# Odd layer of a hybrid decoder trunk: TensorE's order fixed as written, wider distances in the inversion, top priority for the recurrence

## The chip, the cores and the metric

The kernel runs on one core of one Trainium2 chip. The metric is device time in microseconds (us) of one launch. The kernel before takes 2293.18 us (median of 3 runs, 2288.69 to 2293.35). A difference of 0.2%, about 4.6 us, is what can be told from no change here.

## The reference

The model is a two-layer trunk on a sequence of 1024 tokens with 1024 channels. Layer 0 (even) holds dilated attention and an HGRN2 recurrence; the change does not touch it. Layer 1 (odd) is a gated DeltaNet: a projection to q, k (8 heads of 128) and v (16 heads of 128), a causal convolution over 4 steps and SiLU, then the chunked delta rule, a gated RMS norm and an output projection.

```python
def gated_delta_rule_chunked(q, k, v, g, beta):
    ...
    lower = jnp.where(strict, jnp.einsum('bhnid,bhnjd->bhnij', kb, kc) * decay, 0.0)
    a_mat = lower + jnp.eye(C_CHUNK, dtype=jnp.float32)
    sol = lax.linalg.triangular_solve(a_mat, rhs, left_side=True, lower=True, unit_diagonal=True)
    ...
    def step(state, inp):
        u_n, w_n, a_n, qd_n, kt_n, gl_n = inp
        v_new = u_n - jnp.einsum('bhcd,bhdv->bhcv', w_n, state)
        o = jnp.einsum('bhcd,bhdv->bhcv', qd_n, state) + jnp.einsum('bhij,bhjv->bhiv', a_n, v_new)
        new_state = state * gl_n[..., None, None] + jnp.einsum('bhcd,bhcv->bhdv', kt_n, v_new)
        return new_state, o
```

For each k head and each chunk a unit lower triangular matrix is inverted, and then a recurrence runs over the chunks. The kernel uses chunks of 128 tokens, so 8 of them, and does the two v heads that share a k head together.

## The kernel before

The odd layer works through 8 heads. Three kinds of work belong to a head `hh`:

- **Projections, the fill.** `proj(j)` yields the output gate of head j-2 (`way_out`, tiles `oz`, from j = 2 on), and the convolved projections of k of head j+1 (`pk`, absent for j = 7), v of head j (two, `pv`) and q of head j (`pq`). Each projection has two halves of 512 tokens; a half is 24 matmuls on TensorE, then a chain of ScalarE and VectorE passes (`conv`, lines 822 to 831: copy, scale, three multiply-adds, tanh, one more multiply-add). Transposes (`tk`, `tq`, `tv`, `ot`) follow half a projection later. A step of fill is 6 matmuls and is counted in the code as 1.3.
- **Inversion.** `invert(hh)` computes k times k transposed in two parts (`kk`, line 986), turns them into `L` on VectorE (line 992) with decays that ScalarE makes, and inverts the 32 by 32 diagonal blocks on VectorE: a transpose `Lp` (line 1001), 31 dependent pairs of passes `tm` and `Tp` (lines 1007 and 1009), the transposes `Tn` and `Un` (lines 1011 and 1013). Then six small groups of matmuls put the blocks together: `qp`, `up`, two of `q2` (shown as `q`, line 1053) and two of `u2` (shown as `u`, line 1061), each with a copy from PSUM between it and the next.
- **Recurrence.** `recur(hh)` has three parts for a chunk: `ks` and `qs` (matmuls with the state) with the passes `r` on VectorE and `oq` on ScalarE; `vp` with `vt` on VectorE and `vn` on ScalarE; `kv`, `op` and the next chunk's `qk` with the state `S`, `A` and `bv` on VectorE. Each part needs the one before it.

Python generators weave these together. `mix(recur(hh), fill, 2.8)` puts steps of fill worth 2.8 between two parts of the recurrence, and `blend(invert(hh + 1), fill, 0.8)` puts steps worth 0.8 times a written distance between the parts of the next head's inversion. The distance is the first number of each `yield` in `invert`. So, while the recurrence of head hh runs, the projections and the inversion of head hh+1 are the fill.

This fixes the order in which instructions are emitted, and that is only a preference. The framework's scheduler orders each engine's queue when the program is built: of the instructions that are ready by its own estimate of the time, it takes the one that was emitted first. In the attention of the even layer TensorE's order is already kept as emitted, by a region `tc.manual_schedule(engines={PE})`; in the odd layer it is not.

PSUM banks are shared by tag: two for projections (`pj`), two for transposes (`a`), two for `ks`, `kv` and `op` (`b`), one for the inversion's results (`c`) and one for `qk`, `qs` and `vp` (`d`).

The start of the layer is special. `invert(0)` is woven into the end of the gates and `proj(0)` and is emitted before the first head's loop.

Of the kernel before, what the change touches and what calls it, by code (L numbers as in the profile page):

```python
# [9 lines left out]
F32 = mybir.dt.float32  # L10
F32R = mybir.dt.float32r
BF16 = mybir.dt.bfloat16
I32 = mybir.dt.int32
AF = mybir.ActivationFunctionType
ALU = mybir.AluOpType
# [63 lines left out]
def trunk_kernel(ctx: ExitStack, tc: tile.TileContext, x, ew, ewo, ow, owab, owo, nw, fnw, lbl, hnw,  # L79
# [11 lines left out]
    def bank(tag, shape, name):  # L91
        return pp.tile(shape, F32, name=name, tag=tag, bufs=BANKS[tag])
# [79 lines left out]
    def drain(fill):  # L172
        for _ in fill:
            pass
# [565 lines left out]
    def odd_layer(es):  # L740
# [199 lines left out]
        def way_out(hh):  # L940
            normed(hh)
            w = unit()
            for e in range(2):
                yield from gate(hh, w, e, lambda h, g: gated(hh, e, h, g))
# [22 lines left out]
        def invert(hh):  # L967
# [14 lines left out]
            for h in range(2):  # L982
                kk = bank("c", [P, 4, 128], f"kk{hh}_{h}")
                for c in range(4 * h, 4 * h + 4):
                    k_ = kT[:, c * 128:(c + 1) * 128]
                    pe.matmul(kk[:, c - 4 * h, :], k_, k_, start=True, stop=True)
                for c in range(4 * h, 4 * h + 4):
                    gcB = ahead_l.pop()
                    if c < NT - 1:
                        ahead_l.append(decay_l(c + 1))  # L990
                    for e in range(2):
                        dve.scalar_tensor_tensor(L[:, 2 * c + e, :], kk[:, c - 4 * h, :], SC[hh][:, 0, c, e:e + 1],
                                                 gcB[:, e, :], op0=ALU.mult, op1=ALU.mult)
                yield (15 if h else 7.0), 0.9


            for b in range(4):
# [32 lines left out]
                    pe.matmul(qp[a0[r], u, :], L[b0[r], u, a0[r]], Un[b0[r], u, :], start=True, stop=True)  # L1030
            act.copy(Q_[a0[0], :, 0:32], qp[a0[0]])
            dve.tensor_copy(Q_[a0[1], :, 0:32], qp[a0[1]])
            yield 1.5, 1.3
            up = bank("c", [P, 16, 32], f"up{hh}")
            for u in range(16):
                for r in range(2):
# [8 lines left out]
                r = slice(32 * b, 32 * b + 32)  # L1045
                pool.tensor_copy(U[r, :, r], Un[r])

            yield 2.0, 1.8
            for h in range(2):

                q2 = bank("c", [P, 4, 64], f"q2{hh}_{h}")
                for u in range(8 * h, 8 * h + 8):
                    pe.matmul(q2[u % 2 * 64:u % 2 * 64 + 64, u // 2 % 4, :], L[64:128, u, 0:64], U[64:128, u, 64:128],
                              start=True, stop=True)
                for e in range(2):
                    (act.copy if h ^ e else dve.tensor_copy)(Q_[0:64, 8 * h + e:8 * h + 8:2, :], q2[64 * e:64 * e + 64])
                yield 1.2, 1.7
            for h in range(2):
                u2 = bank("c", [P, 4, 64], f"u2{hh}_{h}")
                for u in range(8 * h, 8 * h + 8):  # L1060
                    pe.matmul(u2[u % 2 * 64:u % 2 * 64 + 64, u // 2 % 4, :], T64[:, u, :], Q_[0:64, u, :], start=True, stop=True)
                for e in range(2):
                    d = U[0:64, 8 * h + e:8 * h + 8:2, 64:128]
                    if h ^ e:
                        act.mul(d, u2[64 * e:64 * e + 64], -1.0)
                    else:
                        dve.tensor_scalar(d, u2[64 * e:64 * e + 64], -1.0, None, op0=ALU.mult)
                yield 1.2, 1.7
            dve.memset(U[64:128, :, 0:64], 0.0)
            US[hh] = U  # L1070

        def recur(hh):

            kT, kn, q, bv, U = KT[hh], KN[hh], Q[hh], BV[hh], US[hh]
            ss = SS[hh] = sp.tile([P, NT, 2], F32, name=f"oss{hh}", tag="oss", bufs=2)

            def decay_a(c):
                DA = decays(hh, c, "a")
                pool.tensor_tensor(DA, DA, MA[:, None, :].to_broadcast([P, 2, 128]), op=ALU.add)
                for e in range(2):  # L1080
                    act.activation(DA[:, e, :], DA[:, e, :], AF.Exp, bias=gt["ngc"][:, c, 2 * hh + e:2 * hh + e + 1])
                return DA

            def attend(c):

                DA = ahead_a.pop()
                if c < NT - 1:
                    ahead_a.append(decay_a(c + 1))
                qk = bank("d", [P, 128], f"qk{hh}_{c}")
                s = slice(c * 128, (c + 1) * 128)  # L1090
                pe.matmul(qk, kT[:, s], q[:, s], start=True, stop=True)
                A = sp.tile([P, 2, 128], F32, name=f"A{hh}_{c}", tag="A", bufs=2)
                dve.tensor_tensor(A, qk[:, None, :].to_broadcast([P, 2, 128]), DA, op=ALU.mult)
                return A

            ahead_a = [decay_a(0)]
            yield 1.0
            A = attend(0)
            St = None
            for c in range(NT):  # L1100
                col = [slice(2 * hh + e, 2 * hh + e + 1) for e in range(2)]
                s = slice(c * 128, (c + 1) * 128)
                if c:
                    ks = bank("b", [P, 2, 128], f"ks{hh}_{c}")
                    pe.matmul(ks, kT[:, s], St, start=True, stop=True)
                    r_ = sp.tile([P, 2, 128], F32, name=f"r{hh}_{c}", tag="r")
                    for e in range(2):
                        dve.scalar_tensor_tensor(r_[:, e, :], ks[:, e, :], SC[hh][:, 1, c, e:e + 1],
                                                 bv[:, c, e, :], op0=ALU.mult, op1=ALU.add)
                    qs = bank("d", [P, 2, 128], f"qs{hh}_{c}")  # L1110
                    pe.matmul(qs, q[:, s], St, start=True, stop=True)
                    oq = sp.tile([P, 2, 128], F32, name=f"oq{hh}_{c}", tag="oq")
                    for e in range(2):
                        act.activation(oq[:, e, :], qs[:, e, :], AF.Copy, scale=gt["eg"][:, c, col[e]])
                else:
                    r_ = bv[:, 0]
                yield 1.0
                vp = bank("d", [P, 2, 128], f"vp{hh}_{c}")
                for e in range(2):
                    pe.matmul(vp[:, e, :], U[:, 2 * c + e, :], r_[:, e, :], start=True, stop=True)  # L1120
                if c < NT - 1:
                    vt = sp.tile([P, 2, 128], F32, name=f"vt{hh}_{c}", tag="vt")
                    dve.tensor_tensor(vt, vp, gt["etl"][:, c, 2 * hh:2 * hh + 2, None].to_broadcast([P, 2, 128]), op=ALU.mult)
                vn = sp.tile([P, 2, 128], F32, name=f"vn{hh}_{c}", tag="vn")
                act.copy(vn, vp)
                yield 1.0
                if c < NT - 1:
                    kv = bank("b", [P, 2, 128], f"kv{hh}_{c}")
                    pe.matmul(kv, kn[:, c, :], vt, start=True, stop=True)
                    Sn = sp.tile([P, 2, 128], F32, name=f"S{hh}_{c}", tag="S", bufs=2)  # L1130
                    if c:
                        for e in range(2):
                            dve.scalar_tensor_tensor(Sn[:, e, :], St[:, e, :], gt["egl"][:, c, col[e]],
                                                     kv[:, e, :], op0=ALU.mult, op1=ALU.add)
                    else:
                        dve.tensor_copy(Sn, kv)
                    St = Sn
                op = bank("b", [P, 2, 128], f"op{hh}_{c}")
                for e in range(2):
                    pe.matmul(op[:, e, :], A[:, e, :], vn[:, e, :], start=True, stop=True)  # L1140
                A = attend(c + 1) if c < NT - 1 else None
                if c:
                    dve.tensor_tensor(bv[:, c], op, oq, op=ALU.add)
                else:
                    dve.tensor_copy(bv[:, c], op)
                for e in range(2):
                    jk = sp.tile([P, 128], BF16, name=f"oj{hh}_{c}_{e}", tag="jk", bufs=2)
                    act.activation(jk, bv[:, c, e, :], AF.Square, accum_out=ss[:, c, e:e + 1])
                yield 1.0


# [29 lines left out]
        def seq(*gs):  # L1181
            for g in gs:
                yield from g
# [6 lines left out]
        while 0 not in KN:  # L1190
            next(fill)
        drain(blend(invert(0), fill, 0.8))
        for hh in range(8):
            fill = proj(hh + 1) if hh < 7 else seq(way_out(6), gate7(), out_last(range(3), ["pj"]))
            if hh < 7:
                fill = blend(invert(hh + 1), fill, 0.8)
            mix(recur(hh), fill, 2.8)
            drain(fill)
        nwf = sp.tile([P, D], F32, name="nwf", tag="ub")
        load_row(nwf, fnw)  # L1200
        drain(blend(way_out7(), out_last(range(3, 8), ["pj", "b"])))
# [68 lines left out]
```

## Time and profile before

| what | value |
|---|---|
| median of 3 runs | 2293.18 us |
| the profiled execution | 2290.27 us, span 2288.5 us |
| TensorE busy | 2171.9 us (95%) |
| VectorE busy | 1427.0 us (62%) |
| ScalarE busy | 963.4 us (42%) |
| granted TensorE clock, mean | 0.993 |

The profiled execution lies 2.9 us under the median of the runs. Its span leaves 1.8 us of its own time outside. The odd layer's head loop fills the stretch from about 1294 to 2135 us. In the views, PE is TensorE, DVE is VectorE, ACT is ScalarE; names of tiles appear without their numbers; a window row gives its start and end, its length, then busy time and number of instructions of PE, PEld (weight loads), DVE, ACT and POOL, then the granted TensorE clock, the DMA share and GB/s.

### The profile page before, as it was taken

How to read it: one execution, taken by the hardware profiler on the slowest of the kernel's cores; microseconds unless marked ns; L12 is line 12 of the kernel's file. 1: busy time of each engine (PE TensorE's matmuls, PEld its weight loads, DVE VectorE, ACT ScalarE, POOL GpSimd, SP SyncE). 2: the span in 40 equal slices, each digit the busy share in tenths (PEclk: the TensorE clock that was granted, in tenths of full speed). 3: DMA queues.
4: the chain of work that ended last, by engine and by line, in shares of the span. 5: the costliest groups of instructions: out<-in, count | busy, mean ns of one | idle time of the engine just before them, and what ended most of it. 6: DMA issues, size and time to landing. Idle time of an engine off the chain costs nothing. (4 is left out here: it accounts for less than half of the span.)

```text
span 2288.5 us, 54642 instructions
## 1 busy us (share of the span) xinstructions
PE 2171.9 (95%) x22597; PEld 1809.0 (79%) x22597; DVE 1427.0 (62%) x3364; ACT 963.4 (42%) x2623; POOL 226.5 (10%) x236
## 2 busy tenths in 40 slices
PE   7999999999999999988999988989899989899998
PEld 6888888898888888866887776767777767678787
DVE  6444444444444444456777887878788877855777
ACT  5333333333333332322236663755555555544223
POOL 0000000000000000000000012131212121210000
PEclk9999999999999999999999998999999999999999
DMA  4111111113222323352323221121212121214232
GB/s 145 38 48 48 44 47 48 43 39 95 78 82 84 90 83 92 97 160 88 102 97 104 59 56 62 53 79 46 76 43 76 52 74 59 65 60 148 91 113 109
DMA packets 101864, 175.83 MB, mean 77 GB/s; under 512 B 16752, under 2 KB 34032, under 8 KB 101616
## 3 DMA queue, kind: packets, MB, share of 16 engines
q1 hardware_dynamic: 101616, 172.35, 24.2%
q8 instruction: 177, 2.90, 0.5%
q14 instruction: 71, 0.58, 0.1%
HBM read 127.07 MB, written 25.23 MB: 67 GB/s over the span
## 5 line engine op out<-in xcount | busy, mean ns | idle before, releaser
L113 DVE TENSOR_TENSOR w_lo<-raww,w_hi 128x512 fp32r<-128x512 f32 x292 | 211.9, 727 | 151.1 <-ACT w_hi L112 147.1
L112 ACT CAST w_hi<-raww 128x512 fp32r<-128x512 f32 x292 | 181.1, 620 | 270.1 <-PE op L145 68.0
L143 PE MATMUL av<-w_hi,hn_hi 128*128 128x256 f32 x512 | 149.0, 291 | 0.0
L143 PE MATMUL bi<-w_hi,hn_hi 128*128 128x256 f32 x512 | 147.0, 287 | 0.0
L144 PE MATMUL bi<-w_lo,hn_hi 128*128 128x256 f32 x512 | 145.3, 284 | 0.0
L144 PE MATMUL av<-w_lo,hn_hi 128*128 128x256 f32 x512 | 144.8, 283 | 0.0
L145 PE MATMUL bi<-w_hi,hn_lo 128*128 128x256 f32 x512 | 144.8, 283 | 0.0
L145 PE MATMUL av<-w_hi,hn_lo 128*128 128x256 f32 x512 | 144.7, 283 | 0.0
L575 ACT ACTIVATE P<-P,nm 128x256 f32<-128x256 f32 (+7 forms) x128 | 71.4, 559 | 130.2 <-DVE nm L573 130.0
L143 PE MATMUL op<-w_hi,yplo 128*128 128x512 f32 x288 | 113.5, 394 | 1.6 <-DVE hr L273 0.9
L145 PE MATMUL op<-w_hi,yplo 128*128 128x512 f32 x288 | 112.2, 390 | 0.0
L144 PE MATMUL op<-w_lo,yplo 128*128 128x512 f32 x288 | 112.1, 389 | 0.0
L143 PE MATMUL pv<-hn_hi,w_hi 128*128 128x512 f32 x256 | 107.0, 418 | 2.6 <-ACT uv L822 2.6
L143 PE MATMUL oz<-hn_hi,w_hi 128*128 128x512 f32 x256 | 109.4, 427 | 0.0
L273 DVE TENSOR_TENSOR hr<-hr,op 128x512 f32<-128x512 f32 x128 | 86.1, 684 | 34.5 <-PE op L145 34.0
L145 PE MATMUL pv<-hn_hi,w_lo 128*128 128x512 f32 x256 | 104.3, 407 | 0.0
L144 PE MATMUL pv<-hn_lo,w_hi 128*128 128x512 f32 x256 | 102.6, 401 | 0.0
L144 PE MATMUL oz<-hn_lo,w_hi 128*128 128x512 f32 x256 | 102.3, 400 | 0.0
L145 PE MATMUL oz<-hn_hi,w_lo 128*128 128x512 f32 x256 | 102.0, 398 | 0.0
L581 DVE STREAM_TRANSPOSE PB<-P 128x256 f32<-128x256 f32 (+3 forms) x64 | 54.6, 854 | 74.9 <-ACT P L575 74.8
L143 PEld LDWEIGHTS av<-w_hi,hn_hi 128*128 128x128 f32 x512 | 97.9, 191 | 3.5 <-issue 1.9
L144 PEld LDWEIGHTS bi<-w_lo,hn_hi 128*128 128x128 f32 x512 | 98.1, 192 | 0.0
(354 smaller groups left out, 6044.9 us busy)
## 6 DMA issues: line engine op xcount, KB each, us to landing
raww<-in_ew_dram SPq DMA_DIRECT2D x128, 256.0 KB, 3.1
raww<-in_ow_dram SPq DMA_DIRECT2D x100, 256.0 KB, 3.0
V<-v SPq DMA_DIRECT2D x256, 64.0 KB, 2.0
rawy<-ymix SPq DMA_DIRECT2D x64, 256.0 KB, 2.7
raww<-in_ewo_dram SPq DMA_DIRECT2D x32, 256.0 KB, 3.0
gcl<-gcd SPq DMA_DIRECT2D x64, 128.0 KB, 3.0
gca<-gcd SPq DMA_DIRECT2D x64, 128.0 KB, 3.0
ymix<-oy SPq DMA_DIRECT2D x32, 256.0 KB, 2.0
```

What stands on the lines that cost most here:

```text
L112: act.copy(hi, raw)
L113: dve.tensor_tensor(lo, raw, hi.bitcast(F32), op=ALU.subtract)
L143: pe.matmul(ps, lh, rh, start=start, stop=False)
L144: pe.matmul(ps, lh, rl, start=False, stop=False)
L145: pe.matmul(ps, ll, rh, start=False, stop=stop)
L273: dve.tensor_tensor(dst[:, n], src[:, n], ps, op=ALU.add)
L575: act.activation(Pm[:, e, w0:], Pm[:, e, w0:], AF.Exp, bias=nmx[:, e:e + 1], scale=0.125, accum_out=den[:, i, e:e + 1])
L581: dve.transpose(PB[:, :, i * WG + w0:(i + 1) * WG], Pm[:, :, w0:])
```

## The change

Three edits, all in the odd layer. The number and the shapes of the instructions stay the same.

1. The loop over the heads is put into a region in which TensorE issues its instructions as emitted. The other engines remain the scheduler's. `invert(0)` and what comes before it stay outside.
2. The distances in `invert` grow from 7, 15, 1.5, 2, 1.2 (four times) to 10, 45, 4, 4, 3 (four times).
3. The three parts of each chunk of the recurrence are emitted at the highest priority, so that on the other engines they go ahead of whatever else is ready.

```diff
-                yield (15 if h else 7.0), 0.9
+                yield (45.0 if h else 10.0), 0.9
...
-            yield 1.5, 1.3
+            yield 4.0, 1.3
...
-            yield 2.0, 1.8
+            yield 4.0, 1.8
...
-                yield 1.2, 1.7
+                yield 3.0, 1.7
...
-                yield 1.2, 1.7
+                yield 3.0, 1.7
...
             for c in range(NT):
-                col = [slice(2 * hh + e, 2 * hh + e + 1) for e in range(2)]
...
+                with tc.high_priority():
+                    col = [slice(2 * hh + e, 2 * hh + e + 1) for e in range(2)]
...
+                yield 1.0
+                with tc.high_priority():
+                    vp = bank("d", [P, 2, 128], f"vp{hh}_{c}")
...
+                yield 1.0
+                with tc.high_priority():
+                    if c < NT - 1:
+                        kv = bank("b", [P, 2, 128], f"kv{hh}_{c}")
...
                 yield 1.0
...
-        for hh in range(8):
-            fill = proj(hh + 1) if hh < 7 else seq(way_out(6), gate7(), out_last(range(3), ["pj"]))
-            if hh < 7:
-                fill = blend(invert(hh + 1), fill, 0.8)
-            mix(recur(hh), fill, 2.8)
-            drain(fill)
+        with tc.manual_schedule(engines={mybir.EngineType.PE}):
+            for hh in range(8):
+                fill = proj(hh + 1) if hh < 7 else seq(way_out(6), gate7(), out_last(range(3), ["pj"]))
+                if hh < 7:
+                    fill = blend(invert(hh + 1), fill, 0.8)
+                mix(recur(hh), fill, 2.8)
+                drain(fill)
```

The order of TensorE's work that the new code writes, worked out from the generators (a number after `*` counts steps of 6 matmuls):

```
invert(0), end of proj(0): ... q0*8  qp0 up0 q2 q2 u2 u2   | the region begins
head 0:  kk1.0 k2*2 qk k2*2 tq vp0 k2*2 kv op qk k2*1 kk1.1 k2*1 ks qs v*2 vp v*2 tk kv op qk ...
         ... kv4 op4 qk5 q*1  qp1 up1 ks5 qs5 q2 vp5 q2 u2 kv5 op5 qk6 u2 ks6 qs6 vp6 kv6 op6 qk7 ks7 qs7 vp7 op7
head 1 and later (hh):  kk.0 oz*2 qk oz*2 ot vp0 oz*2 kv op qk oz*1 kk.1 oz*1 ot ks qs oz*2 vp oz*2 ot ...
         ... k*2 kv op qk k*2 tq ... v*1 tk ... v*1 (end of the first v) v*2 ks5 qs5 qp v*1 vp5 v*1 tv v*1 kv op qk up
         v*1 ks6 qs6 v*1 q2 vp6 v*1 q*1 kv op qk q2 ks7 qs7 q*2 u2 vp7 q*1 tv op7 q*1 u2 q*3
```

More of the change, by code (lines that the diff above doesn't have):

```diff
@@ L1100, in recur @@
             for c in range(NT):
-                col = [slice(2 * hh + e, 2 * hh + e + 1) for e in range(2)]
[L1102 to L1106, printed above, removed]
-                    for e in range(2):
[L1108 to L1112, printed above, removed]
-                    for e in range(2):
-                        act.activation(oq[:, e, :], qs[:, e, :], AF.Copy, scale=gt["eg"][:, c, col[e]])
-                else:
-                    r_ = bv[:, 0]
@@ L1117, in recur @@
[L1117 to L1130, printed above, removed]
+                with tc.high_priority():
+                    col = [slice(2 * hh + e, 2 * hh + e + 1) for e in range(2)]
+                    s = slice(c * 128, (c + 1) * 128)
+                    if c:
+                        ks = bank("b", [P, 2, 128], f"ks{hh}_{c}")
+                        pe.matmul(ks, kT[:, s], St, start=True, stop=True)
+                        r_ = sp.tile([P, 2, 128], F32, name=f"r{hh}_{c}", tag="r")
+                        for e in range(2):
+                            dve.scalar_tensor_tensor(r_[:, e, :], ks[:, e, :], SC[hh][:, 1, c, e:e + 1],
+                                                     bv[:, c, e, :], op0=ALU.mult, op1=ALU.add)
+                        qs = bank("d", [P, 2, 128], f"qs{hh}_{c}")
+                        pe.matmul(qs, q[:, s], St, start=True, stop=True)
+                        oq = sp.tile([P, 2, 128], F32, name=f"oq{hh}_{c}", tag="oq")
+                        for e in range(2):
+                            act.activation(oq[:, e, :], qs[:, e, :], AF.Copy, scale=gt["eg"][:, c, col[e]])
+                    else:
+                        r_ = bv[:, 0]
@@ new lines, in recur @@
+                yield 1.0
+                with tc.high_priority():
+                    vp = bank("d", [P, 2, 128], f"vp{hh}_{c}")
+                    for e in range(2):
+                        pe.matmul(vp[:, e, :], U[:, 2 * c + e, :], r_[:, e, :], start=True, stop=True)
+                    if c < NT - 1:
+                        vt = sp.tile([P, 2, 128], F32, name=f"vt{hh}_{c}", tag="vt")
+                        dve.tensor_tensor(vt, vp, gt["etl"][:, c, 2 * hh:2 * hh + 2, None].to_broadcast([P, 2, 128]), op=ALU.mult)
+                    vn = sp.tile([P, 2, 128], F32, name=f"vn{hh}_{c}", tag="vn")
+                    act.copy(vn, vp)
@@ new lines, in recur @@
+                yield 1.0
+                with tc.high_priority():
+                    if c < NT - 1:
+                        kv = bank("b", [P, 2, 128], f"kv{hh}_{c}")
+                        pe.matmul(kv, kn[:, c, :], vt, start=True, stop=True)
+                        Sn = sp.tile([P, 2, 128], F32, name=f"S{hh}_{c}", tag="S", bufs=2)
+                        if c:
+                            for e in range(2):
+                                dve.scalar_tensor_tensor(Sn[:, e, :], St[:, e, :], gt["egl"][:, c, col[e]],
+                                                         kv[:, e, :], op0=ALU.mult, op1=ALU.add)
+                        else:
+                            dve.tensor_copy(Sn, kv)
+                        St = Sn
+                    op = bank("b", [P, 2, 128], f"op{hh}_{c}")
+                    for e in range(2):
+                        pe.matmul(op[:, e, :], A[:, e, :], vn[:, e, :], start=True, stop=True)
+                    A = attend(c + 1) if c < NT - 1 else None
@@ L1131, in recur @@
                     if c:
-                        for e in range(2):
-                            dve.scalar_tensor_tensor(Sn[:, e, :], St[:, e, :], gt["egl"][:, c, col[e]],
-                                                     kv[:, e, :], op0=ALU.mult, op1=ALU.add)
-                    else:
[L1136 to L1148, printed above, removed]
+                        dve.tensor_tensor(bv[:, c], op, oq, op=ALU.add)
+                    else:
+                        dve.tensor_copy(bv[:, c], op)
@@ L1149, in recur @@
+                    for e in range(2):
+                        jk = sp.tile([P, 128], BF16, name=f"oj{hh}_{c}_{e}", tag="jk", bufs=2)
+                        act.activation(jk, bv[:, c, e, :], AF.Square, accum_out=ss[:, c, e:e + 1])
                 yield 1.0
```

## The prediction

> **What bounds the kernel now.** I read the page first, then a row of busy times for each head, then who TensorE waits for.
>
> ```profile
> span 2288.5 us, 54642 instructions
> PE 2171.9 (95%) x22597; PEld 1809.0 (79%) x22597; DVE 1427.0 (62%) x3364; ACT 963.4 (42%) x2623; POOL 226.5 (10%) x236
> ```
>
> TensorE is busy for 95% of the span. The other engines matter only where it waits for them. In the rows by window the length is followed by the busy time of PE, PEld, DVE, ACT and POOL, then the granted clock. The first row is the even layer's attention, the others are the odd layer from the end of `proj(0)` on, each window about one head as TensorE's order has it now.
>
> ```profile
> 550.00:990.00 440.00, 438.25 (x7873) 372.67 (x7873) 207.33 (x553) 133.43 (x368) 13.32 (x7) 1.00 0.32 92
> ...
> 1294.00:1342.00 48.00, 44.91 (x415) 36.12 (x414) 44.26 (x117) 24.70 (x70) 5.83 (x8) 1.00 0.17 53
> 1342.00:1425.00 83.00, 71.38 (x535) 55.72 (x535) 62.76 (x176) 43.05 (x126) 19.85 (x23) 0.92 0.22 61
> 1425.00:1515.00 90.00, 83.29 (x618) 65.76 (x618) 75.18 (x219) 55.30 (x173) 18.44 (x20) 1.00 0.19 55
> 1515.00:1611.00 96.00, 88.16 (x647) 71.57 (x646) 75.96 (x210) 55.61 (x173) 14.17 (x17) 1.00 0.19 59
> 1611.00:1718.00 107.00, 99.34 (x697) 80.56 (x697) 85.02 (x227) 60.62 (x183) 21.31 (x23) 1.00 0.21 63
> 1718.00:1825.00 107.00, 99.91 (x702) 81.10 (x701) 85.56 (x226) 61.28 (x183) 21.16 (x23) 1.00 0.20 62
> 1825.00:1934.00 109.00, 99.78 (x700) 80.63 (x699) 87.36 (x229) 61.96 (x185) 21.29 (x23) 1.00 0.22 66
> 1934.00:2040.00 106.00, 96.19 (x674) 77.59 (x672) 81.94 (x206) 54.20 (x156) 20.94 (x23) 0.98 0.20 61
> 2040.00:2135.00 95.00, 91.61 (x447) 75.49 (x447) 50.89 (x110) 38.46 (x117) 13.13 (x14) 1.00 0.38 130
> ```
>
> Length less PE's busy time gives TensorE's idle time: 3.1, 11.6, 6.7, 7.8, 7.7, 7.1, 9.2, 9.8 and 3.4, together 66.4 us of 841. That is the most the change can win, since it neither adds nor removes an instruction. VectorE is at 80% in a full head (85.56 of 107). The next view says what TensorE waits for there (sum, times, longest).
>
> ```profile
> PE op L1140 <- ACT vn L1125: 12.1, 15, 1.5
> PE vp L1120 <- ACT oq L1114: 8.8, 10, 1.7
> PE ks L1105 <- DVE S L1133: 8.7, 7, 1.8
> PE ot L935 <- POOL bv L928: 5.7, 7, 3.1
> PE kk L986 <- DVE L L992: 5.5, 4, 1.5
> PE q L1053 <- ACT L L1041: 4.9, 6, 2.1
> PE up L1037 <- DVE Q L1032: 4.6, 5, 1.5
> ```
>
> None is long. The scheduler put each of these a little too early for the real delay. `qp`, which needs the whole VectorE inversion, is hardly a wait now, because the present order moves `qp` behind other work until `Un` is there.
>
> **The change, part by part.** I take the written order and ask at which places it makes TensorE wait. The rows for this are TensorE's and VectorE's order at the first head (start, duration), two inversions from `Lp` to `Un` (1446.89 to 1493.89, 1742.22 to 1775.54), the `kk` groups of a full head, and its VectorE groups (sum, mean in ns).
>
> ```profile
> 1292.98 0.39 PE L144 MATMUL pq<-hn_lo,w_hi 128*128 128x512 f32 x1
> 1293.20 0.39 PE L145 MATMUL pq<-hn_hi,w_lo 128*128 128x512 f32 x1
> ...
> 1299.14 1.03 PE L840 MATMUL tq<-ident,q 128*128 128x128 f32 x8
> 1323.12 1.20 PE L1030 MATMUL qp<-Un,L 32*32 32x32 f32 x64 [0.48 <-DVE rt L190]
> ...
> 1331.64 0.68 PE L1053 MATMUL q<-L 64*64 64x64 f32 x16
> 1334.34 0.68 PE L1053 MATMUL q<-L 64*64 64x64 f32 x16
> ...
> 1338.19 0.38 PE L1120 MATMUL vp<-bv,L 128*128 128x128 f32 x2
> ...
> 1299.23 0.28 DVE L1009 TENSOR_TENSOR Tp<-Tp,tm 128x126 f32<-128x126 f32 x1
> ...
> 1446.89 2.03 DVE L1001 STREAM_TRANSPOSE Lp<-Lg 128x1024 f32<-128x1024 f32 x1 [0.22 <-ACT Lg L999]
> ...
> 1493.89 0.70 DVE L1013 STREAM_TRANSPOSE Un<-Tn 128x512 f32<-128x512 f32 x1
> ...
> 1742.22 2.02 DVE L1001 STREAM_TRANSPOSE Lp<-Lg 128x1024 f32<-128x1024 f32 x1 [1.77 <-ACT Lg L999]
> ...
> 1775.54 0.68 DVE L1013 STREAM_TRANSPOSE Un<-Tn 128x512 f32<-128x512 f32 x1
> ...
> 1718.02 1.05 PE L986 MATMUL kk<-kT 128*128 128x128 f32 x8
> ...
> 1728.36 1.16 PE L986 MATMUL kk<-kT 128*128 128x128 f32 x8 [1.26 <-DVE L L992]
> ...
> L1007 DVE TENSOR_TENSOR tm<-Lp,Tp 128x126 f32<-128x126 f32 (+22 forms) x31 | 9.4, 303 | 0.7
> L827 DVE SCALAR_TENSOR_TENSOR vT<-uv,cws,vT 128x512 f32<-128x512 f32 x12 | 9.2, 771 | 0.8 <-ACT vT L825 0.5
> L1009 DVE TENSOR_TENSOR Tp<-Tp,tm 128x126 f32<-128x126 f32 (+22 forms) x31 | 8.8, 285 | 0.6
> ```
>
> *First head.* Before, `proj(0)` ends at 1293.4, `qp` of `invert(0)` runs at 1323 and the first `vp` at 1338. In those 45 us TensorE stays busy (3.1 us idle) because it takes on the k, v and most of the q projections of `proj(1)`. In the written order only four steps, `kk`, `qk` and `tq` stand ahead of the first `vp`: 24 matmuls at the 0.23 us between the two `pq` rows, 5.5 us, and about 2 us of small ones. TensorE runs dry near 1301. `Tp` at 1299.23 is pair 11 of 31 (its 126 columns are 21 rows of 6). With VectorE almost to itself, 40 passes of 0.29 us and some 0.04 between them are 13 us, part of a conv chain 2, `Tn` and `Un` 2: `qp` near 1317. After it come `qp` (1.2), a copy, `up` (1.2), copies of both engines and three groups of 0.68 with copies, about 9 us in all, so `vp` starts near 1326. TensorE works 4.4 us of that and idles 20. Against the 3.1 of before that is +17. If `invert(0)`, now emitted behind the convs of `proj(0)`, is no earlier than before (1338), it is +29; if VectorE gets through its list sooner, +9. I take 17, the middle of the count, and 2 for the clock (below): **+19**.
>
> *Rest of head 0.* `proj(1)` has no output gate: 8 halves are 41.6 units of fill, and the inversion of head 1 asks for 8 and 36 ahead of its `qp`. So the fill ends just ahead of `qp`, and chunks 5 to 7 follow with nothing between their parts. Before, the scheduler put `oz` of head 0 there. Some ten hand-offs now stand bare; the present waits are 0.8 to 1.2 us each (12.1 in 15, 8.7 in 7), a part of which the neighbouring small groups hide, so 3 to 12 us, taken as 6.5. The distance from the second `kk` to `qp` is also shorter than in later heads, for 5 to 8 us of `qp` waiting. Together 14 against 11.6: **+3** (-4 to +12).
>
> *Six heads.* Between two parts of the recurrence stand 2.8 units of fill, 13 matmuls, 3 us. The longest present wait on such a part is 1.8 us, and with priority the passes no longer stand behind convs. I count these waits as gone, and those of `kk`, `up` and `q` too (3 to 4 units instead of 1.2 to 2, with recurrence between). What is late next is `qp`, because nothing can pass it now. From the second `kk` to `qp` stand 28 of the head's 48 steps, 39 us. The head's other work on TensorE is 34 us (99.91 less 48 steps of 1.38), and 4.7 of 8 chunks with the transposes between, some 14 us, fall into this stretch. The first `kk` lies 14 us ahead (7 steps and a chunk's part or two), so `qp` comes 67 us after it. `Lp` comes 24 us after the first `kk` (1718.02 to 1742.22) and some 2 later with the wider distance. That leaves 40.5 us for the inversion. It takes 34.0 us where VectorE has few convs beside it (1742.22 to the end of `Un`, 1776.22) and 47.7 where four halves of convs run there (1446.89 to 1494.59). The written order puts k and the first v, four halves, just there, all emitted ahead of the inversion's passes, and the recurrence ahead of everything. So `qp` is late by 0 to 7 us. VectorE's list there is 21 us of inversion (9.4, 8.8 and 2.0 in the groups, 0.7 for `Un`), 12 of convs (four halves of three passes at 0.77 and one like them) and its share of everything else: 85.56 less 21 and 24 for a head's eight halves leaves 41, of which 38% falls here, 15. That is 48 us, were none of it put off behind `Un`. The last half's passes can be, so I take 43.5, nearer to the second row, which the stretch resembles: 3 us late. With 2 us of other hand-offs (a conv chain that is not through when its transposes come, 1 us; small ones) a head idles 5 us, and the last of the six, whose fill ends early, 2 more: 32 against 48.3 (6.7 to 9.8 above). **-16**, bounds -36 (2 us a head) and +24 (12 us a head).
>
> *Last head.* It has fill enough and no inversion; `ot` and `tq` still wait: **-1**.
>
> *The clock.* After the gaps at the end of head 0 TensorE ran at half its clock:
>
> ```profile
> 1399.30:1412.90 13.60, 11.29 (x171) 8.37 (x174) 8.88 (x15) 4.41 (x7) 9.46 (x11) 0.50 0.20 67
> ```
>
> That stretch cost up to 6.8 us. The 20 us hole at the first head may start another: 0 to 6.8, taken as 2, since projections follow the hole at once, while in this row transposes and `qp` did. [...]
>
> *Other queues.* The loads of the decays for the recurrence move ahead on SP, and their additions ahead on GpSimd (POOL is busy 21 of 107 us). Nothing in the view of waits puts TensorE behind a weight load, so I cost this at nothing; without that cover it would be a weight tile late by one such load.
>
> **The sum.** 19 + 3 - 16 - 1 = +5 us. The profiled execution took 2290.27 us and becomes 2295; the runs' median is 2.9 above it, and I forecast the median: 2293.2 + 5 = 2298.
>
> **The rivals.**
>
> 1. *The inversion is in time and the fixed order wins: faster.* For it: in attention, where the order is fixed too, TensorE idles 1.75 of 440 us; VectorE has 20% to spare. Against it: VectorE is at 47% there. If `qp` is on time and a head idles 2.5 us, the six heads give -33, and 19 + 3 - 33 - 1 = -12: 2281. It decides from `qp` being late by under 1 us a head.
> 2. *VectorE becomes the bound at each `qp`: much slower.* If the inversion takes the full 47.7 us, `qp` is 7 us late, a head idles 9 to 10 and drops to half clock for some microseconds after it: 6 times +3.5 and 12 of clock, with 22 - 1 of the start: +54, 2347. For it: the inversion at 1446.89. Against it: that stretch held a larger share of convs and later ones. [...]
> 3. *The hole of the first head does not come*, because the scheduler brings `invert(0)` to its end sooner. Against it: VectorE was busy 44.26 of 48 us there. It gives 19 less: 2280.
> 4. *The parts cancel*: 2289 to 2298.
>
> **How the numbers follow.** The forecast (slower by 5 to 30, its own range 2298 to 2323) has 0.37, rivals 1 and 3 together 0.38, rival 2 0.10, cancelling 0.15. A measurement tells 0.2%, 4.6 us, from no change, so slower is 0.37 + 0.10 = 0.47, same 0.15, faster 0.38. The two signs lie close: the terms of the sum are +19 and -16, and either can be off by its own size. The range leaves out one in ten on each side: from 2270 (six heads near their lower bound) to 2332 (short of rival 2).
>
> **What would show it.** Right: one idle stretch of 12 to 30 us ahead of the first `vp` with `u2`'s copy as its end; `qp` <- `Un` as the longest wait, about 3 us in each of six heads; `op` <- `vn`, `vp` <- `oq`, `ks` <- `S` together under 8 us (29.6 now); bare hand-offs at the end of head 0. Wrong: a full head shorter than 102 us, or the first `vp` before 1315.

## The result and the profile after

The changed kernel takes 2349.07 us (median of 4 runs, 2344.55 to 2353.56) against 2292.90 for the kernel before: 1.0249 times as long, 95% interval 1.0223 to 1.0276. The profiled execution took 2346.06 us, 55.8 more than the one before.

The page of the changed kernel: TensorE's busy time grows by 11.5 us, so the other 44 us of the longer span are idle time.

```profile
span 2344.3 us, 54679 instructions
...
PE 2183.4 (93%) x22597; PEld 1827.3 (78%) x22597; DVE 1448.9 (62%) x3364; ACT 963.9 (41%) x2623; POOL 228.2 (10%) x236
```

Busy times by window of the changed kernel, with the columns as before. The first row goes from the end of `proj(0)` to the first matmul of the region, the next two are the rest of head 0, then come full heads (two left out), the last of the six and the last head.

```profile
1293.00:1329.00 36.00, 8.57 (x225) 7.58 (x226) 23.25 (x68) 4.90 (x10) 4.09 (x7) 0.54 0.07 23
1329.00:1390.00 61.00, 56.71 (x269) 47.46 (x270) 40.67 (x112) 36.22 (x117) 3.52 (x4) 0.91 0.22 53
1390.00:1446.00 56.00, 32.91 (x326) 25.93 (x325) 35.74 (x94) 17.00 (x50) 7.84 (x11) 0.66 0.09 24
1446.00:1554.00 108.00, 100.02 (x694) 81.74 (x694) 84.55 (x226) 59.37 (x184) 19.87 (x23) 0.98 0.19 58
1554.00:1662.00 108.00, 99.81 (x700) 81.22 (x699) 88.21 (x225) 60.95 (x183) 22.01 (x23) 1.00 0.21 62
...
1878.00:1986.00 108.00, 99.57 (x701) 81.19 (x700) 88.82 (x224) 62.15 (x185) 21.77 (x23) 1.00 0.25 67
1986.00:2096.00 110.00, 98.50 (x670) 80.13 (x669) 83.02 (x209) 53.54 (x155) 23.27 (x25) 0.94 0.20 60
2096.00:2191.00 95.00, 92.84 (x454) 76.56 (x453) 52.30 (x111) 39.16 (x118) 10.89 (x12) 1.00 0.38 128
```

Length less PE's busy time again gives the idle time. Beside the same stretches before:

| stretch | idle before | idle after | difference | forecast |
|---|---|---|---|---|
| `proj(0)` to the region's first work | 3.1 | 27.4 | +24.3 | +17 |
| rest of head 0 | 11.6 | 27.4 | +15.8 | +3 |
| six heads | 48.3 | 52.0 | +3.7 | -16 |
| last head | 3.4 | 2.2 | -1.2 | -1 |
| TensorE's busy time, all of these | 774.6 | 789.1 | +14.5 | +2 |

The differences add up to 57 us. The waits of TensorE in the changed kernel (sum, times, longest) say which work is late:

```profile
PE qp L1030 <- DVE Un L1013: 35.3, 2, 20.0
PE vp L1122 <- ACT oq L1115: 32.0, 24, 2.4
PE kv L1132 <- DVE vt L1125: 8.0, 10, 0.9
```

`qp` waits 35.3 us in two places only, which the order in time shows: at 1312 (head 0's own inversion) and at 1415 (head 1's, at the end of head 0). In a full head `qp` does not wait: `Un` ends at 1621.9 and `qp` goes at 1626.8, when its turn comes. (A row with fewer than the 64 matmuls of a `qp` group comes from a view that ends inside the group.)

```profile
1292.00 0.39 PE L145 MATMUL pq<-hn_hi,w_lo 128*128 128x512 f32 x1
...
1312.34 1.86 PE L1030 MATMUL qp<-Un,L 32*32 32x32 f32 x62 [19.95 <-DVE Un L1013]
...
1328.74 2.07 PE L986 MATMUL kk<-kT 128*128 128x128 f32 x8 [0.94 <-DVE L L1067]
...
1415.90 1.33 PE L1030 MATMUL qp<-Un,L 32*32 32x32 f32 x42 [15.34 <-DVE Un L1013]
...
1621.22 0.70 DVE L1013 STREAM_TRANSPOSE Un<-Tn 128x512 f32<-128x512 f32 x1
...
1626.83 0.85 PE L1030 MATMUL qp<-Un,L 32*32 32x32 f32 x42
```

The third row is what the forecast had missed at the start. The region's first instruction is `kk` of head 1. It needs PSUM tag `c`, and that one bank serves `qp`, `up`, `q2` and `u2` of `invert(0)` until 1328. The row names its releaser, the last copy out of that bank (`L`, line 1067). Everything in the region stands behind it, so not even the 24 matmuls that the forecast let run at 1293 did.

Over most of the two holes and on into the work behind them the granted clock is half (the third column from the end, 0.50 for 37.5 us each time):

```profile
1295.70:1333.20 37.50, 12.77 (x239) 11.20 (x240) 21.71 (x65) 3.87 (x8) 4.09 (x7) 0.50 0.04 11
1404.90:1442.40 37.50, 20.84 (x260) 16.51 (x260) 21.10 (x57) 8.43 (x26) 5.29 (x9) 0.50 0.07 18
```

There the matmuls of a projection start 0.43 us apart (1331.46 and 1331.89) instead of 0.23 (1289.73 and 1289.96). An estimate from that: the clock cost at most half of the 33.6 us that TensorE was busy there, 17 us, against up to 6 in the 13.6 us stretch before: up to 11 of the +14.5. Shorter stretches (3.4 to 10.2 us) add to it: the windows of the head loop show 102 us at half clock in all, 75 of them in these two, against 17 us before.

The second stretch ends before any projection runs:

```profile
1438.55 1.22 PE L1132 MATMUL kv<-vt,kn 128*128 128x256 f32 x2 [0.52 <-DVE vt L1125]
...
1441.70 1.00 PE L1112 MATMUL qs<-S,q 128*128 128x256 f32 x2
1443.48 0.71 PE L1122 MATMUL vp<-r,L 128*128 128x128 f32 x4 [0.78 <-ACT oq L1115]
...
1446.07 0.48 PE L143 MATMUL oz<-hn_hi,w_hi 128*128 128x512 f32 x1
```

### The profile page after: what moved, and what is told of

Its sections match the earlier page's. It is cut to its first block, busy times and chain, and to the rows that moved or that the text cites. A ratio compares the mean times of both kernels' runs of the same rounds, so it can differ in the third digit from the quotient of the medians.

```text
span 2344.3 us, 54679 instructions
## 1 busy us (share of the span) xinstructions
PE 2183.4 (93%) x22597; PEld 1827.3 (78%) x22597; DVE 1448.9 (62%) x3364; ACT 963.9 (41%) x2623; POOL 228.2 (10%) x236
## 5 line engine op out<-in xcount | busy, mean ns | idle before, releaser
L145 PE MATMUL pv<-hn_hi,w_lo 128*128 128x512 f32 x256 | 101.8, 398 | 0.0
```

What stands on the lines that cost most here:

```text
L145: pe.matmul(ps, ll, rh, start=False, stop=stop)
```

## The experiments

Each time stands beside runs of the kernel before on the same chip (medians of 2289.2 to 2293.3 us). In brackets are the ratio to these and its 95% interval.

**The three edits one by one.** First the region alone, and the region and the priority with the old distances; then the changed kernel without the priority, the priority alone and the distances alone.

Region alone, as an edit of the kernel before:

```diff
+        with tc.manual_schedule(engines={mybir.EngineType.PE}):
             for hh in range(8):
```

> The kernel before with the region of fixed TensorE order over all heads as its only edit (old distances, no priority). By the run with the old distances and the priority (2466.15 us) the inversion is late at every qp: 2450 to 2485 us. Rival: the priority of the recurrence kept VectorE from the inversion there, and without it qp waits only half as long: under 2420 us.

Measured: 2436.90 us (1.0633, 1.0603 to 1.0663). Region and priority with the old distances, as an edit of the changed kernel:

```diff
-                yield (45.0 if h else 10.0), 0.9
+                yield (15 if h else 7.0), 0.9
...
```

> The changed kernel with the old distances (7, 15, 1.5, 2, 1.2). The hole at the first head shrinks, since invert(0) is woven in earlier by some 12 us of fill, but qp now comes some 24 units of fill earlier in every head while the inversion takes 34 to 42 us from Lp to Un: from Lp to qp are then about 15 us, so TensorE waits some 20 to 25 us at qp in each of six heads. 2420 to 2490 us. Rival: if the scheduler's VectorE order is what sets the inversion, and it goes faster where qp is earlier, at most 10 us a head: 2350 to 2400 us.

Measured: 2466.15 us (1.0747, 1.0720 to 1.0774). The waits over five full heads of the two, in this order:

```profile
PE qp L1030 <- DVE Un L1013: 96.2, 5, 19.3
```

```profile
PE qp L1030 <- DVE Un L1013: 101.8, 5, 20.8
```

So the fixed order with the distances of before waits some 20 us for the inversion in every head, and the wider distances take that wait away. This is the rule that the forecast rested on, and it is right; the priority hardly changes this wait (96.2 and 101.8). The run with the priority is 29 us longer all the same. The waits at `qp` explain some 7 of that over all heads, and the rest is not resolved here.

Changed kernel without the priority:

```diff
-                with tc.high_priority():
+                if True:
```

> The changed kernel without the highest priority. Theory 'start': the holes at the first head stay, so within 12 us of the changed kernel (2349 us); in the full heads the wait of vp for oq (25.5 us in five heads) shrinks if the priority of the decays causes it, and waits of vp, ks and kv for VectorE grow. 2337 to 2360 us. Rival 'priority': the priority is what cost the time, then under 2310 us.

Measured: 2346.86 us (1.0223, 1.0205 to 1.0242), level with the changed kernel. TensorE's wait of `vp` for `oq` over five full heads, in the changed kernel and in this run:

```profile
PE vp L1122 <- ACT oq L1115: 25.5, 18, 2.4
```

```profile
PE vp L1122 <- ACT oq L1115: 13.1, 6, 2.6
```

In exchange `kv`, `ks` and `op` wait 22.2 us together instead of 11.8. Priority alone, with the scheduler's order and the old distances, as an edit of the kernel before:

```diff
             for c in range(NT):
+                with tc.high_priority():
...
```

> The kernel before with the highest priority for the recurrence's parts as its only edit. TensorE's order is the scheduler's, so nothing holds back borrowed work and there is no hole at the first head. The recurrence waits less for VectorE (op for vn 12.1, ks for S 8.7) but the exponentials of the decays block ScalarE more: 2280 to 2300 us. Rival: the priority alone is worth the 30 us of these waits: under 2275 us.

Measured: 2308.02 us (1.0078, 1.0055 to 1.0100), slower than expected. TensorE does not idle more (60.9 us from 1294 to 2150, against 66.4 before), it runs slower. A full head, and the wait that goes with it over the head loop:

```profile
1727.10:1835.60 108.50, 102.05 (x700) 81.43 (x699) 86.95 (x224) 61.40 (x183) 20.06 (x23) 0.98 0.20 62
```

```profile
PE qp L1030 <- DVE Un L1013: 13.5, 7, 3.0
```

A wait of up to 3 us at `qp` now comes in most heads, the mean clock is 0.98, and the matmuls of a head are busy for 102.05 us instead of 99.91. In the windows by head from 1342 to 2049 the mean clock is 0.91, 0.96 and five times 0.98; before, it was 0.92, five times 1.00 and 0.98. With the decays taken out of the priority and emitted behind each chunk:

```diff
                 DA = ahead_a.pop()
-                if c < NT - 1:
-                    ahead_a.append(decay_a(c + 1))
...
+            ahead_a.append(decay_a(1))
...
+                if c < NT - 2:
+                    ahead_a.append(decay_a(c + 2))
```

> The kernel before with the highest priority for the recurrence's parts, but the decays' loads and passes at plain priority. With all of it at the highest priority it takes 2308.02 us, with 20 us more of TensorE's busy time than before (half clock) and no more idle time. Theory 'decays': they block ScalarE; without them 2290 to 2297 us. Rival 'order': the scheduler's TensorE order with the recurrence first leaves qp to be waited for (13.5 us in 7 waits, each followed by half clock), decays or not: 2303 to 2313 us.

Measured: 2304.93 us (1.0070, 1.0057 to 1.0083). So the decays are not what the priority costs in a free order. The order that comes of it is the likelier cause: the waits at `qp` are there in this run too (15.3 us in 5, against 13.5 in 7 with the decays in the priority and 2.3 in 2 before). That they come of the order was not tested by itself. Distances alone, as an edit of the kernel before:

```diff
-                yield (15 if h else 7.0), 0.9
+                yield (45.0 if h else 10.0), 0.9
...
```

> The kernel before with the wider distances as its only edit. With a free order a distance is only a preference, so qp goes when Un is there: 2288 to 2305 us. Rival: the inversion falls behind the convs on VectorE, the next head's first vp is late and TensorE idles at the heads' ends: above 2310 us.

Measured: 2288.54 us (0.9988, 0.9975 to 1.0001), no difference that can be told.

**Where the region begins.** The loop over the heads was split, with head 0, or heads 0 and 1, ahead of the region:

```diff
+        heads(range(1))
         with tc.manual_schedule(engines={mybir.EngineType.PE}):
-            for hh in range(8):
+            heads(range(1, 8))
```

> The changed kernel, but its region of fixed TensorE order starts at head 1 and not at head 0. Theory 'start': nearly all of the loss (42.6 us of idle time and 14.5 us of busy time at half clock in the stretch from proj(0) to the last head) lies at the first head: 24 us in the hole ahead of its first vp, 16 us at its bare end, the rest clock. With head 0 left to the scheduler the hole goes; the bare end stays in part, because the region's first matmul (kk of head 2) waits for the one bank of the inversion, so that no gate of head 0 can be pulled into chunks 5 to 7. 2305 to 2325 us. Rival 'steady': the fixed order or the priority costs in every head; then it stays above 2335 us.

Measured: 2329.19 us (1.0145, 1.0124 to 1.0167), a little over the expected.

> The changed kernel with the region starting at head 2. Theory 'start': head 0 now borrows work from head 1 as in the kernel before, so the bare end goes too; the full heads keep their 8 us of idle time each: 2290 to 2300 us. Rival 'steady': above 2335 us. If it is above the run with the region from head 1, the wide distances and not the fixed order cost at the first head.

Measured: 2323.98 us (1.0125, 1.0107 to 1.0143). Both theories missed: 25 us of the loss went, the rest stayed. With the region from head 1, `qp` waits 21.5 us at the inversion of head 1. With the region from head 2, TensorE's order shows a new hole, now at the inversion of head 2:

```profile
1512.74 1.49 PE L1030 MATMUL qp<-Un,L 32*32 32x32 f32 x47 [17.41 <-DVE Un L1013]
...
1529.15 2.07 PE L986 MATMUL kk<-kT 128*128 128x128 f32 x8 [0.94 <-DVE L L1067]
```

In the stretch of this hole (1435.8 to 1529.1) TensorE idles 29.0 us, against 6.7 in that head before: 22 of the 31 us that stayed.

The hole goes with the start of the region, whichever head that is. Ahead of it the free part uses up its own work; everything behind stands in the chain whose first link, the second row, waits for the inversion's bank. What is special about head 0 is only the second hole.

**The first link.** The changed kernel, with `kk` of head 1 in another bank:

```diff
-                kk = bank("c", [P, 4, 128], f"kk{hh}_{h}")
+                kk = bank("b" if hh == 1 else "c", [P, 4, 128], f"kk{hh}_{h}")
```

> The changed kernel, with kk of head 1 alone in a bank of tag b, so that the region's first matmul does not wait for the bank that invert(0) holds. Theory 'chain behind one bank': kk, 24 matmuls of the k projection, qk and the transposes of q then run in the hole ahead of qp of head 0, 7 to 8 us of work, and what stood behind the hole starts that much earlier: the first vp 7 to 9 us earlier, 2336 to 2343 us. Rival: the scheduler still puts these matmuls behind u of head 0, or VectorE gets slower by as much as TensorE gains: 2344 us and more.

Measured: 2342.18 us (1.0227, 1.0208 to 1.0247), as expected. In TensorE's order `kk` now goes at 1291.69, ahead of the hole:

```profile
1291.69 0.94 PE L986 MATMUL kk<-kT 128*128 128x128 f32 x7
...
1316.61 1.60 PE L1030 MATMUL qp<-Un,L 32*32 32x32 f32 x52 [17.24 <-DVE Un L1013]
```

The hole stays 17.24 us long: after the 24 matmuls, `qk` and `tq` the chain's next link is `vp`, which needs the whole inversion.

**The holes' length and the full heads.** The changed kernel with 15 of the 31 pairs of passes:

```diff
-            for k in range(31):
+            for k in range(15):
```

> The changed kernel with 15 of the 31 pairs of passes in the inversion on VectorE (the inverses are incomplete; only the time is read). This takes 32 passes, about 8 us, from VectorE in each head, and 8 to 10 us from the chain ahead of each qp. Theory 'holes are the inversion': both holes of the first head shrink by that much each and with them the half clock: 20 to 30 us less than 2349. Theory 'VectorE's load makes the hand-offs late': a full head's idle time falls from 8 to 4 us or less, another 20 us: together 2295 to 2310 us. Rival 'static order': the full heads keep 7 to 8 us of idle time, because the passes of recurrence stand in the queues behind others whatever the load: 2318 to 2330 us.

Measured: 2316.73 us (1.0120, 1.0107 to 1.0134), 32 us less than the changed kernel and just under the range of the last reading. The two holes of the first head, and a full head:

```profile
1306.36 1.86 PE L1030 MATMUL qp<-Un,L 32*32 32x32 f32 x62 [10.70 <-DVE Un L1013]
...
1395.33 1.86 PE L1030 MATMUL qp<-Un,L 32*32 32x32 f32 x62 [2.90 <-DVE Un L1013]
```

```profile
1637.20:1744.20 107.00, 100.35 (x700) 82.70 (x699) 80.52 (x193) 60.99 (x183) 21.60 (x23) 0.98 0.20 62
```

The holes shrink by 9.3 and 12.4 us, so they are the inversion's passes. The full heads keep 5.8 to 6.7 us of idle time, against 7.5 to 8.4 in the changed kernel, with 7 to 8 us less on VectorE: its load accounts for a small part of the recurrence's waits.

**What keeps them.** ScalarE's and then TensorE's order in a full head of the changed kernel:

```profile
1600.64 0.70 ACT L1081 ACTIVATE gca<-gca,g_ngc 128x128 f32<-128x128 f32 x2 [2.71 <-POOL gca L1079]
...
1602.99 0.76 ACT L825 ACTIVATE kT<-uk,cws 128x512 f32<-128x512 f32 x1
1603.61 0.66 ACT L1115 ACTIVATE oq<-qs,g_eg 128x128 f32<-128x128 f32 x2
...
1604.32 0.60 PE L1122 MATMUL vp<-r,L 128*128 128x128 f32 x3 [2.44 <-ACT oq L1115]
```

ScalarE stands 2.71 us before the exponential of a decay that is needed only a chunk later, then does squares and a conv copy, then `oq`; `vp` waits for `oq` because it shares the bank with `qs`. Two edits on the run with the region from head 2 take these apart: `qs` in another bank, and the decays at plain priority (the edit shown above).

```diff
-                        qs = bank("d", [P, 2, 128], f"qs{hh}_{c}")
+                        qs = bank("b", [P, 2, 128], f"qs{hh}_{c}")
```

> The run with the region from head 2 (2323.98 us), and qs in the two banks of tag b instead of the one bank of tag d that it shares with vp. Theory 'bank': in the fixed order vp follows qs in the same bank and must wait until oq has emptied it (25.6 us in 18 waits in five heads); with another bank that wait goes, vp waits for r alone, and a full head idles 3 to 4 us instead of 8: 20 to 28 us less, 2296 to 2304 us. Rival 'late passes': ScalarE's queue is what is late, and the wait goes over to op for vn and to kv: less than 8 us better, above 2316 us.

> The run with the region from head 2, and the decays of the recurrence (their load, GpSimd's addition, ScalarE's two exponentials) emitted behind each chunk at plain priority. Theory 'priority inversion': at top priority these exponentials stand in ScalarE's queue long before their data come (71.8 us of waiting there in five heads of the changed kernel, 28.5 in four before), and oq stands behind them; at plain priority oq is in time: 12 to 22 us less than 2323.98. Rival 'bank': the order of ScalarE's other work (squares of tq, conv copies) keeps oq late all the same: within 6 us of 2323.98.

> Both edits on the run with the region from head 2. If both causes are real and not the same one: 24 to 32 us less than 2323.98, about 2296. What stays then over the kernel before is the hole at the start of the region (17.4 us at qp, 7 us of bare copies and the half clock after it).

Measured: 2322.78 (1.0142, 1.0120 to 1.0165), 2312.67 (1.0096, 1.0077 to 1.0114) and 2312.14 us (1.0091, 1.0072 to 1.0111). TensorE's waits over five heads, without an edit, with the bank and with the decays:

```profile
PE vp L1122 <- ACT oq L1115: 24.2, 15, 2.7
PE kv L1132 <- DVE vt L1125: 5.8, 7, 0.9
```

```profile
PE kv L1132 <- DVE vt L1125: 10.6, 14, 1.0
PE vp L1122 <- DVE r L1109: 10.3, 14, 1.1
```

```profile
PE vp L1121 <- ACT oq L1114: 10.2, 10, 2.4
PE vp L1121 <- DVE r L1108: 6.4, 9, 1.0
```

With another bank the wait for `oq` is gone and 10 us for `r` and 5 more for `vt` stand in its place; the kernel is no faster. With the decays behind the chunk at plain priority more than half of it goes and 11 us are won, a little under what was expected. Only part of the 11 us lies in these heads: over the five TensorE idles 38.4 us instead of 44.1. Both together are no better than the second alone. The edit changes the place of the decays as well as their priority, and the run without any priority had the wait of `vp` smaller and the time level.

**In the scheduler's order.** The bank alone, and the bank with the wider distances, on the kernel before:

> The kernel before, with qs in the banks of tag b and nothing else. Its vp waits for oq 8.8 us in the odd layer. If this wait goes without a new one: 2281 to 2288 us. Rival: the scheduler uses the freedom to move vp and op earlier still and waits as much for vn, ks or S: 2289 to 2297 us.

> The kernel before with the wider distances and with qs in the banks of tag b, in the scheduler's order and without priority. The distances alone were level (ratio 0.9988), the bank alone too (0.9992). With the distances vp waits 17.2 us for oq in the head loop, which the bank takes away: 2278 to 2288 us. Rival: the waits change their name as they did in the fixed order: 2286 to 2294 us.

Measured: 2290.13 (0.9992, 0.9982 to 1.0003) and 2284.40 us (0.9977, 0.9967 to 0.9988). The second is faster than both kernels, by little. One of its full heads idles 5.1 us instead of 7.1; with the distances alone it is 5.5:

```profile
1722.00:1827.00 105.00, 99.93 (x698) 80.51 (x697) 86.46 (x223) 60.05 (x182) 21.82 (x23) 1.00 0.22 64
```

## Why the prediction was wrong

The time, 2349.07, lies outside the range of 2270 to 2332. Rival 2 gave 2347, but by a mechanism that did not occur, `qp` late by 7 us in every full head, so its nearness is luck. Its 12 us of clock over six heads is a term that no run shows: with waits of some 19 us at `qp` (region alone) a full head, 1570.40 to 1694.20, had a mean clock of 0.92 and TensorE busy for 101.24 us against 99.91 before, by which six heads make an estimated 8 us. The hole at the first head came, and so did the bare hand-offs behind it, both larger than forecast. The gain in the full heads, which was to pay for them, did not come at all: this step of the forecast failed, and it is the largest of the four misses below (20 us of 52).

- *Six heads*, -16 forecast, +3.7 measured. Two steps failed. `qp` was never late: the inversion took 41.6 us (1580.3 to 1621.9, as the forecast's 43.5 nearly had it), but the stretch left it 46 and not 40.5. And the waits of the recurrence were counted as gone because 3 us of fill stand between its parts. `op` for `vn`, `vp` for `oq` and `ks` for `S` were to be under 8 us together. They came to 38.6 over the head loop, against 29.6 before, 32.0 of them `vp` for `oq`. The distance is between TensorE's instructions. What fills it on the other engines is their own queues, and ScalarE's held an exponential whose data were not there. With these exponentials emitted later and at plain priority that wait fell from 24.2 to 10.2 in five heads. Priority is not all of it: without any priority ScalarE still waits 91.0 us at them (1290 to 2150; 104.5 in the changed kernel), and the time is the same.
- *Rest of head 0*, +3 forecast, +15.8 measured. Its parts were right in kind and sized too small. The wait at `qp` was put at 5 to 8 us and was 15.3, since `Lp` to `Un` took 48 us there (1368.0 to 1415.8). The other 12.1 us of the 27.4 stand against 6.5 for the bare hand-offs.
- *The clock*, +2 forecast, +14.5 of busy time measured, up to 11 of it, by the estimate above, in the two long stretches at half clock. The prediction let the half clock end soon because projections were to follow the hole at once, which was the author's estimate; no run shows its 2 us. But its own count puts 9 us from `qp` to `vp` between, and even the stretch before that it leaned on has projections at half clock, from 1407.3 to 1411.5. In the run `qp` to `u2` took 16 us of small matmuls with gaps, and the clock stayed at half until 1333.2, when 4.5 us of unbroken work, `kk` and 2.7 us of projections, had passed since the last idle time. The second stretch ends 3.9 us after the last idle time, with small matmuls alone; yet an unbroken run of such matmuls from 1429.4 to 1436.0 lies inside it at half clock. What ends such a stretch is not shown here. The forecast also had no half clock in the full heads, where waits of 2.36 and 2.34 us at `vp` were each followed by 3.4 us of it (last section).
- *First head*, +17 forecast, +24.3 measured. The count let `kk`, 24 matmuls, `qk` and `tq` run ahead of the hole. It looked at the written order alone and not at the PSUM bank that the first of them needs. The run with that `kk` in another bank had the forecast's picture, dry near 1300 and `qp` at 1316.6, and was 6.9 us shorter. Its `vp` came at 1330.5 and not at 1326, because `qp` to `vp` took 14 us instead of 9.
- *Last head* and *other queues* came as forecast: -1.2 us, and no wait of TensorE for a weight among its waits (1190 to 2344, down to 0.5 us in total).
- *Rival 1* leaned on the attention stage, where the fixed order idles 1.75 of 440 us. The comparison did not carry over.

One question stays open: why a full head idles 5 to 9 us in every version tried in which `qp` is in time, fixed order or free. Half the passes on VectorE, the other bank and the later decays each take off 1 to 2 us a head and leave the rest.

## What to carry to other kernels

A fixed order takes from the scheduler the right to borrow: ask of the order's first instruction, and of the first one that needs a long chain, what could run instead, and look for the buffers it needs and not only for the data. Distances written for a full stage have to be held against the stage that has less fill; here the one stage with less fill idled 16 us more, and the six full ones won nothing. Whether a priority on a chain should cover what merely prepares a later step has to be tried: moving the decays out of it and behind the chunk won 11 us in the fixed order and nothing that can be told in the free one.

## What the runs showed of the hardware

In the changed kernel TensorE's clock stayed at half for 37.5 us twice. In the first stretch (1295.70 to 1333.20) TensorE was busy for 12.77 us, in groups of small matmuls 0.9 to 2.1 us apart and then in unbroken work for 4.5 us; in the second (1404.90 to 1442.40) for 20.84 us, in small matmuls of which many followed each other without a gap. A group of 64 `qp` matmuls that took 1.20 us at the full clock (1323.12 in the kernel before) took 1.92 us in both. Half clock came after short waits too. In the changed kernel waits of 2.36 and 2.34 us at `vp` (1496.4 and 1820.3) were each followed by 3.4 us at half clock, while one of 2.44 us at 1604.3 was not. With the priority in a free order, where `qp` waited 7 times for up to 3.0 us, the mean clock of a full head was 0.98 (1727.10 to 1835.60), and its matmuls were busy for 102.05 us instead of 99.91.
